# Score products of a two-layer backbone: two batches of small matmuls a head in place of four, three adaLN steps behind each

## The chip, the cores and the metric

The kernel runs on one core of a Trainium2 chip. The metric is the device time of one execution in microseconds (us), the median of several runs. The engines are named as the profile names them: PE is TensorE's matmul, PEld its weight load, DVE is VectorE, ACT is ScalarE, POOL is GpSimd, SP is SyncE, which issues the weight DMAs.

## The reference

A latent stream of 512 tokens and a context of 256 tokens go through two layers of width 1024. Each layer normalises, applies an adaLN modulation (shift, scale, gate from a conditioning vector), runs a mixer that is 2048 wide, and adds the gated result. Layer 0 is a bidirectional HGRN2 recurrence with 16 heads of 128 channels, layer 1 a bidirectional RG-LRU. The change touches layer 0 alone:

```python
q, v, zf, zb, g = jnp.split(hh @ w_in, 5, axis=-1)
f = lb + (1.0 - lb) * jax.nn.sigmoid(z)          # forget gate, one per direction; key = 1 - f
scores = jnp.einsum('bhtk,bhsk,bhtsk->bhts', qc, kc, decay)
o = einsum('bhts,bhsv->bhtv', scores, vc) + einsum('bhtk,bhkv->bhtv', qc * exp(b), S)
S = exp(b_last) * S + einsum('bhsk,bhsv->bhkv', kc * exp(b_last - b), vc)
shift, scale, gate = jnp.split(silu(c) @ ada_w[i] + ada_b[i], 3, axis=-1)
```

## The kernel before

All 768 tokens are kept with channels on the partitions, in 6 chunks of 128. The big projections are done in fp32 split into a high and a low part, three matmuls per product (lines 311 to 313; line 381 for v). A weight tile of 512 KB arrives by DMA in one of three `raw` buffers, ACT rounds it to `hi` (line 129), and DVE takes the rest as `lo` (line 130).

Inside a head the decayed scores of a chunk come from a tree of 7 levels (`NLEV`). At level l the blocks of B = 2^l tokens are paired, and the matmuls of `products` multiply the keys of one block with the queries of its neighbour, decayed up to their border. `KK` holds the keys and `QQ` the queries of both directions, and behind each level DVE multiplies both in place by decay products `T` (lines 502 and 509). `kt` is a gathered copy of KK on ACT (line 416). An odd level also gathers the queries, into `qt` (lines 416, 490, 491), and an even one reads QQ in place. Levels 0 to 5 take 24 matmuls of 128x32 each, level 6 takes 12 of 128x64. They use a part of PE's columns each (`tile_position`), while every other matmul of the head uses the whole array. `dg`, also 24 small matmuls, is the diagonal.

The four batches of a head are dg with level 0, levels 1 and 2, levels 3 and 4, levels 5 and 6. Each product has its own PSUM bank out of a pool of four (`aps`), from which the tiles `ada`, `adat`, `kT`, `U`, `o` and `pm` also come. `scores` moves products away: DVE's copy_predicated into D for levels 0 to 4 (line 468), ACT copies into `A` for levels 5 and 6 (line 473, 4 and 2 of them), and four copies from D into A (line 477).

`interleave` runs head h together with a filler, mostly the input projections (`in_0` to `in_3`) of head h+1. In odd heads the filler also has the v projection for two heads, in even heads from 2 on the output projection `o`. `prep` gathers level 0's `kt_0` of the next head ahead of that head, and makes its kd and QQ.

`ada_block` is the side work. One block has four steps of 4 matmuls (line 230), each on a 512 KB weight tile of its own; with the fourth ACT copies the bank to `blk` (line 236), then PE transposes it (`adat`, line 240) and DVE adds. The side work has two blocks in heads 0 and 1 and six in heads 9 to 14. Behind each of the four batches stands `next(side)`, one step; what is left of a block runs at the head's end.

The order on each engine is set by a scheduler that works on the recorded program: within each engine, instructions run in the order that it leaves, and a waiting one holds up those behind it. Names in the rows: `lv_5` is level 5's bank, `kT` the transposed keys, `hi`, `lo` and `raw` weights, `sg` a sigmoid, `h_hi` and `h_lo` the normalised input.

Of the kernel before, what the change touches and what calls it, by code (L numbers as in the profile page):

```python
# [9 lines left out]
AF = mybir.ActivationFunctionType  # L10
# [3 lines left out]
P = 128  # L14
# [7 lines left out]
NC = NT // P  # L22
# [22 lines left out]
def view(t, off, dims):  # L45
    a = t[:]
    if isinstance(a, Nothing):
        return a
    return bass.AP(tensor=a.tensor, offset=a.offset + off, ap=[a.ap[0]] + [list(d) for d in dims])
# [119 lines left out]
def build(tc, ins, out, plan):  # L169
    nc = tc.nc  # L170
    PE, V, A = nc.tensor, nc.vector, nc.scalar
# [7 lines left out]
    def dtile(name):  # L179
        return dps.tile([P, 512], F32, name=name, tag="d")  # L180

    def atile(name):
        return aps.tile([P, 512], F32, name=name, tag="a")
# [135 lines left out]
    l0 = ExitStack()  # L319
    p0 = lambda name, bufs=1: l0.enter_context(tc.tile_pool(name=name, bufs=bufs))  # L320
    qp, kdp, tp, ap_, sp, rp = p0("qp"), p0("kdp"), p0("tp"), p0("ap"), p0("sp"), p0("rp")
    qqp, kkp, gsp, ktp, qtp = p0("qqp", 2), p0("kkp", 2), p0("gsp", 2), p0("ktp", 3), p0("qtp", 2)
    vp, tmp = p0("vp", 3), p0("tmp", 4)
    halves = (slice(0, HN), slice(HN, NT))
    st = [{} for _ in range(NH)]
# [4 lines left out]
    def tmpt(name):  # L330
        return tmp.tile([P, HN], F32, name=name, tag="tmp")
# [81 lines left out]
    def gather(KK, kt, B):  # L413

        n = NT // (2 * B)
        A.activation(view(kt, 0, [[2 * B, n], [B, 2], [1, B]]), view(KK, 0, [[2 * B, n], [NT + B, 2], [1, B]]), AF.Copy)  # L416
# [12 lines left out]
    def hgrn(h, side):  # L429

        s = st[h]
        KK, QQ, kt = s["KK"], s["QQ"], s["kt"]
        At = ap_.tile([P, NC, P], F32, name=f"A{h}", tag="A")
        D = tmpt(f"D{h}").rearrange("p (c t) -> p c t", t=64)[:, :, :32]

        dg = atile(f"dg{h}")
        for c in range(NC):
            for g in range(4):  # L440
                t = slice(P * c + 32 * g, P * c + 32 * g + 32)
                PE.matmul(dg[32 * g:32 * g + 32, 32 * c:32 * c + 32], lhsT=s["kd"][:, t], rhs=s["q"][:, t],
                          start=c == 0, stop=c == NC - 1, skip_group_check=True, tile_position=(0, 32 * g))

        def products(l, kt, qt):
            B = 1 << l
            ps = atile(f"lv{h}_{l}")
            w = 64 if B == 64 else 32
            for c in range(NC):
                for g in range(P // w):  # L450
                    o = P * c + w * g
                    if qt is not None:
                        rhs = qt[:, o:o + w]
                    elif B < 32:
                        rhs = view(QQ, o, [[2 * B, 16 // B], [NT + B, 2], [1, B]])
                    elif g % 2 == 0:
                        rhs = QQ[:, 1, o + w:o + 2 * w]
                    else:
                        rhs = QQ[:, 0, o - w:o]
                    PE.matmul(ps[w * g:w * g + w, w * c:w * c + w], lhsT=kt[:, o:o + w], rhs=rhs, start=c == 0,  # L460
                              stop=c == NC - 1, skip_group_check=True, tile_position=(0, w * g))
            return ps

        def scores(l, ps):
            w = 64 if l == 6 else 32
            psv = ps[:, :w * NC].rearrange("p (c t) -> p c t", c=NC)
            if l < 5:
                V.copy_predicated(D, masks[:, l][:, None, :].to_broadcast([P, NC, 32]), psv)
            else:
                for g in range(P // w):  # L470
                    q = slice(w * g, w * g + w)
                    k = slice(w * (g ^ 1), w * (g ^ 1) + w)
                    A.activation(At[q, :, k], psv[q], AF.Copy)
            if l == 4:
                for g in range(4):
                    q = slice(32 * g, 32 * g + 32)
                    A.activation(At[q, :, q], D[q], AF.Copy)

        T = s["T0"]
        waiting = None  # L480
        for l in range(NLEV):
            B = 1 << l
            n = NT // (2 * B)
            m = NT // B
            first = l % 2 == 1
            if first:
                qt = qtp.tile([P, NT], F32, name=f"qt{h}_{l}", tag="qt")
                if B == 32:

                    A.activation(view(qt, 0, [[2 * B, n], [1, B]]), view(QQ, NT + B, [[2 * B, n], [1, B]]), AF.Copy)  # L490
                    A.activation(view(qt, B, [[2 * B, n], [1, B]]), view(QQ, 0, [[2 * B, n], [1, B]]), AF.Copy)  # L491
                else:
                    gather(QQ, qt, B)
                waiting = (l, kt, qt)
            else:
                pss = [(waiting[0], products(*waiting))] if waiting else []
                pss.append((l, products(l, kt, None)))
                next(side, None)
                if l == 0:
                    A.activation(D, dg[:, :32 * NC].rearrange("p (c t) -> p c t", c=NC), AF.Copy)  # L500
            kv = view(KK, 0, [[2 * B, n], [NT + B, 2], [1, B]])
            V.tensor_tensor(kv, kv, view(T, 1, [[2, n], [m - 1, 2], [0, B]]), ALU.mult)  # L502
            if l < NLEV - 1:
                kt = ktp.tile([P, NT], F32, name=f"kt{h}_{l + 1}", tag="kt")
                gather(KK, kt, 2 * B)
            T2 = tp.tile([P, 2, n], F32, name=f"T{l + 1}_{h}", tag=f"T{l + 1}")
            V.tensor_tensor(T2, view(T, 0, [[m, 2], [2, n]]), view(T, 1, [[m, 2], [2, n]]), ALU.mult)
            qv = view(QQ, 0, [[2 * B, n], [NT + B, 2], [1, B]])
            V.tensor_tensor(qv, qv, view(T, m + 1, [[2, n], [-m - 1, 2], [0, B]]), ALU.mult)  # L509
            if not first:  # L510
                for x in pss:
                    scores(*x)
            T = T2
            yield 4.0 - 0.3 * l + (1.5 if l == 0 else 0)

        for dr, cs in ((0, (0, 1, 2)), (1, (0, 1)), (0, (3, 4)), (1, (3, 4, 5))):
            ps = atile(f"kT{h}_{dr}_{cs[0]}")
            for i, c in enumerate(cs):
                PE.matmul(ps[:, P * i:P * i + P], lhsT=KK[:, dr, P * c:P * c + P], rhs=ident, is_transpose=True,
                          start=i == 0, stop=i == len(cs) - 1, skip_group_check=True)  # L520
# [7 lines left out]
        for part in ((0, 3), (3, 5)):  # L528
            for dr in range(2):
                ps = atile(f"U{h}_{dr}_{part[0]}")  # L530
                for i in range(part[0], part[1]):
                    c = chain[dr][i]
                    PE.matmul(ps[:, P * (i - part[0]):P * (i - part[0]) + P], lhsT=KK[:, dr, P * c:P * c + P],  # L533
                              rhs=Vt[:, c], start=i == part[0], stop=i == part[1] - 1, skip_group_check=True)
                for i in range(part[0], part[1]):
# [3 lines left out]
                    else:  # L539
                        c = chain[dr][i]  # L540
# [9 lines left out]
        parts = halves if h < NH - 1 else segs  # L550
        pos, sqs = [], []
        for half, c_ in enumerate(parts):
            ps = atile(f"o{h}_{half}")
            cs = range(c_.start // P, c_.stop // P)
            pos.append(ps[:, :P * len(cs)])
            for i, c in enumerate(cs):
                t = slice(P * c, P * c + P)
# [6 lines left out]
                for j, (a, b) in enumerate(ops):  # L564
                    PE.matmul(po, lhsT=a, rhs=b, start=i == 0 and j == 0, stop=c == cs[-1] and j == len(ops) - 1,  # L565
                              skip_group_check=True)
# [17 lines left out]
        for half, c in enumerate(parts):  # L584
            g = s["gs"][:, c]
# [52 lines left out]
    wi, first = {}, {}  # L638
# [52 lines left out]
    def chain_(gens):  # L691
        for g in gens:
            yield from g
# [13 lines left out]
    def extra(h):  # L707
        if h in (1, 2):
            return [ada_block(0, 3 + h)]
        return [ada_block(1, h - 10)] if h >= 10 else []  # L710

    for h in range(NH):
        if h == 0:
            fill, total = [v_item(0), in_item(0, 3), head_in(1)], 54700.0
        elif h < NH - 1:
            fill, total = [head_in(h + 1)], 45300.0 if h < NH - 2 else 23500.0
        else:
            fill, total = [in_item(h, 3), out_item((h - 3, h - 2, h - 1))], 31400.0
        side = chain_(extra(h + 1) if h < NH - 1 else [])
        interleave(hgrn(h, side), HW, chain_(fill), total)  # L720
        run_all(side)
# [13 lines left out]
    first = [[(w, dtile(f"rc{e}")[:, :CTX]) for e, w in enumerate(wx)]]  # L735
# [172 lines left out]
    s = rt[j]  # L908
# [7 lines left out]
    pss = []  # L916
    for d in range(DK):
        ps = (dtile if d < 4 else atile)(f"ro{j}_{d}")
# [14 lines left out]
    for i in range(2):  # L933
        c = slice(H * i, H * i + H)
        cx = slice(CTX + H * i, CTX + H * i + H)
        for d in range(DK):
            ps = pss[d][:, c] if d < 5 else (dtile if i else atile)(f"ro{j}_{d}_{i}")[:, :H]
# [6 lines left out]
    for i, rs in enumerate(rsf):  # L944
        c = slice(H * i, H * i + H)
        cx = slice(CTX + H * i, CTX + H * i + H)
        for k in range(DK):
            o = fin[i][k // 4][:, k % 4]
# [81 lines left out]
```

## Time and profile before

| | |
|---|---|
| runs | 1584.18, 1584.83, 1586.97 us; median 1584.83 |
| profiled execution | 1585.53 us, span 1583.7 us, granted clock 0.986 of full speed on average |
| PE busy | 1530.8 us, 97% of the span |
| PEld, DVE, ACT, POOL busy | 90%, 76%, 57%, 1% |
| chain of work that ended last | PE 87%, DVE 8%, ACT 2% |

The span runs from the first to the last instruction. The profiled execution took 0.70 us more than the median and 1.8 us more than its own span. Heads 2 to 14 last about 63 us each: head 9's dg begins at 651.85 us and head 10's at 717.70.

### The profile page before, as it was taken

To read this page: it belongs to the slowest core of one execution; us is meant where nothing else is said; L and a number is where in the kernel's file an instruction comes from. 1 tells how busy PE (TensorE), PEld (TensorE's weight loads), DVE (VectorE), ACT (ScalarE), POOL (GpSimd) and SP (SyncE) were. 2 spreads that over 40 slices of the span, in tenths; PEclk is the share of its full clock that TensorE was granted. 3 is DMA by queue.
4 is the path that set the end of the run, shared out by engine and by line. 5 is a ranking of instruction groups with operands and counts; after the bars stand their busy time and mean duration, and the time that the engine had idled before them with its cause. 6 is when DMAs were issued, how large, how long until landed. Compare 5 with 4: busy or idle time off the path is not lost.

```text
span 1583.7 us, 34061 instructions
## 1 busy us (share of the span) xinstructions
PE 1530.8 (97%) x14740; PEld 1429.7 (90%) x14740; DVE 1208.6 (76%) x1867; ACT 903.9 (57%) x1423; POOL 11.8 (1%) x16
## 2 busy tenths in 40 slices
PE   5999999999999999999999999998999999999995
PEld 3899999999999999999999999987888888888884
DVE  4767678768867878767866876787668797797898
ACT  4554554555544554554445555654578577667874
POOL 0000000000000000000000000001000000000001
PEclk9999999999999999999999999998999999999997
DMA  8231211111211211223222131201222212221211
GB/s 317 91 121 54 95 55 41 55 54 30 80 41 42 68 45 51 81 69 103 70 92 73 54 120 56 94 15 54 66 68 67 89 59 67 94 78 59 76 54 53
DMA packets 33861, 116.80 MB, mean 74 GB/s; under 512 B 3632, under 2 KB 6064, under 8 KB 33712
## 3 DMA queue, kind: packets, MB, share of 16 engines
q1 hardware_dynamic: 32192, 113.26, 22.5%
q8 instruction: 116, 1.90, 0.5%
q10 hardware_dynamic: 1520, 1.37, 0.3%
q14 instruction: 33, 0.27, 0.1%
HBM read 112.52 MB, written 2.10 MB: 72 GB/s over the span
## 4 chain that ended last, share of the span: by engine, by line
PE 87%; DVE 8%; ACT 2%; issue 1%; POOL 0%; DMA 0%; POOLq 0%; DVEq 0%; ACTq 0%
PE in L311 12%; PE in L312 11%; PE in L313 11%; PE v L381 9%; PE lv L460 4%; PE o L565 4%; PE r L313 3%; PE r L311 3%; PE r L312 3%; PE o L311 3%; PE o L312 3%; PE o L313 3%; PE U L533 2%; PE gt L311 2%; PE gt L312 2%; PE gt L313 2%
## 5 line engine op out<-in xcount | busy, mean ns | idle before, releaser
L311 PE MATMUL in<-h_hi,hi 128*128 128x384 f32 x1024 | 350.4, 343 | 3.4 <-ACT h_hi L304 2.8
L312 PE MATMUL in<-h_lo,hi 128*128 128x384 f32 x1024 | 345.8, 338 | 0.3 <-DVE h_lo L305 0.3
L313 PE MATMUL in<-h_hi,lo 128*128 128x384 f32 x1024 | 344.6, 337 | 0.0
L130 DVE TENSOR_TENSOR lo<-raw,hi 128x1024 fp32r<-128x1024 f32 x160 | 195.8, 1225 | 85.9 <-ACT hi L129 85.6
L129 ACT ACTIVATE hi<-raw 128x1024 fp32r<-128x1024 f32 x160 | 168.1, 1057 | 110.5 <-PE in L312 49.3
L311 PEld LDWEIGHTS in<-h_hi,hi 128*128 128x128 f32 x1024 | 192.9, 189 | 16.8 <-issue 9.9
L312 PEld LDWEIGHTS in<-h_lo,hi 128*128 128x128 f32 x1024 | 193.1, 189 | 2.8 <-issue 1.6
L313 PEld LDWEIGHTS in<-h_hi,lo 128*128 128x128 f32 x1024 | 192.6, 188 | 0.8 <-issue 0.4
L509 DVE TENSOR_TENSOR QQ<-QQ,T 128x768 f32<-128x768 f32 x112 | 117.7, 1051 | 20.7 <-ACT qt L491 20.5
L313 PE MATMUL r<-h_hi,lo 128*128 128x512 f32 (+1 forms) x344 | 123.8, 360 | 3.8 <-DVE lo L130 3.8
L416 ACT ACTIVATE kt<-KK 128x768 f32<-128x768 f32 x112 | 102.5, 915 | 40.8 <-DVE KK L502 33.1
L502 DVE TENSOR_TENSOR KK<-KK,T 128x768 f32<-128x768 f32 x112 | 117.3, 1047 | 9.7 <-ACT kt L416 8.2
L312 PE MATMUL r<-h_lo,hi 128*128 128x512 f32 (+1 forms) x344 | 123.1, 358 | 0.0
L311 PE MATMUL r<-h_hi,hi 128*128 128x512 f32 (+1 forms) x344 | 123.0, 358 | 0.0
L337 ACT ACTIVATE sg<-in 128x384 f32<-128x384 f32 x128 | 61.5, 482 | 100.7 <-PE in L313 100.5
L381 PE MATMUL v<-hi,h_hi 128*128 128x256 f32 x384 | 111.3, 290 | 0.0
L381 PE MATMUL v<-hi,h_lo 128*128 128x256 f32 x384 | 107.4, 280 | 0.0
L381 PE MATMUL v<-lo,h_hi 128*128 128x256 f32 x384 | 107.3, 279 | 0.0
L588 DVE RECIPROCAL sq<-sq 128x384 f32<-128x384 f32 x30 | 76.3, 2546 | 21.1 <-ACT sq L582 20.9
L405 DVE SCALAR_TENSOR_TENSOR x<-o,ada,x 128x256 f32<-128x256 f32 (+1 forms) x184 | 82.1, 486 | 11.3 <-PE o L313 10.8
L311 PE MATMUL o<-rhi,hi 128*128 128x384 f32 (+2 forms) x240 | 85.3, 357 | 1.8 <-DVE lo L130 1.2
L311 PE MATMUL gt<-xh,hi 128*128 128x384 f32 x256 | 85.6, 337 | 0.8 <-ACT xh L790 0.4
(207 smaller groups left out, 3280.1 us busy)
## 6 DMA issues: line engine op xcount, KB each, us to landing
raw<-in_hgw_dram SPq DMA_DIRECT2D x64, 512.0 KB, 3.6
raw<-in_ada_dram SPq DMA_DIRECT2D x48, 512.0 KB, 3.8
raw<-in_rgi_dram SPq DMA_DIRECT2D x32, 512.0 KB, 3.9
raw<-in_hgv_dram SPq DMA_DIRECT2D x16, 512.0 KB, 3.5
raw<-in_hgo_dram SPq DMA_DIRECT2D x16, 512.0 KB, 3.6
raw<-in_rgg_dram SPq DMA_DIRECT2D x16, 512.0 KB, 3.6
raw<-in_rgo_dram SPq DMA_DIRECT2D x16, 512.0 KB, 3.9
x<-in_x_dram SPq DMA_DIRECT2D x8, 384.0 KB, 5.9
```

What stands on the lines that cost most here:

```text
L129: self.nc.scalar.activation(hi, r, AF.Copy)
L130: self.nc.vector.tensor_tensor(lo, r, hi.bitcast(F32), ALU.subtract)
L311: PE.matmul(ps, lhsT=wh, rhs=xh, start=first and i == 0, stop=False, skip_group_check=skip)
L312: PE.matmul(ps, lhsT=wh, rhs=xl, start=False, stop=False, skip_group_check=skip)
L313: PE.matmul(ps, lhsT=wl, rhs=xh, start=False, stop=last and i == n - 1, skip_group_check=skip)
L381: PE.matmul(ps, lhsT=xh[:, kk, t], rhs=w[:, k], start=part == 0 and k == 0 and i == 0 and c % 2 == 0, stop=part == 1 and k == 3 and i == 2 ...
L405: V.scalar_tensor_tensor(xs, ps[:, a - c.start:b - c.start], gate[:, d, 1 - j:2 - j], xs, ALU.mult, ALU.add)
L416: A.activation(view(kt, 0, [[2 * B, n], [B, 2], [1, B]]), view(KK, 0, [[2 * B, n], [NT + B, 2], [1, B]]), AF.Copy)
L460: PE.matmul(ps[w * g:w * g + w, w * c:w * c + w], lhsT=kt[:, o:o + w], rhs=rhs, start=c == 0, stop=c == NC - 1, skip_group_check=True, til ...
L502: V.tensor_tensor(kv, kv, view(T, 1, [[2, n], [m - 1, 2], [0, B]]), ALU.mult)
L509: V.tensor_tensor(qv, qv, view(T, m + 1, [[2, n], [-m - 1, 2], [0, B]]), ALU.mult)
L588: V.reciprocal(rs, rs)
```

## The change

The products of a head now come in two batches. The first is the diagonal with levels 0, 1 and 2, in two PSUM banks; the second is levels 3 to 6, in three banks: levels 3 and 4 share one, level 5 and level 6 have one each. Levels 0, 1, 3, 4 and 5 gather their queries into a `qt`; levels 2 and 6, the last of each batch, read QQ. So there are two more gathers a head on ACT. The buffers of `kt` go from 3 to 5, those of `qt` from 2 to 3. Behind each batch stand up to three steps of the side work. The scores of a batch are moved away behind the level on which it ended. Line numbers behind line 440 move by up to 10: line 460 becomes 459, 468 becomes 467, 473 becomes 472.

```diff
-    qqp, kkp, gsp, ktp, qtp = p0("qqp", 2), p0("kkp", 2), p0("gsp", 2), p0("ktp", 3), p0("qtp", 2)
+    qqp, kkp, gsp, ktp, qtp = p0("qqp", 2), p0("kkp", 2), p0("gsp", 2), p0("ktp", 5), p0("qtp", 3)
...
-        def products(l, kt, qt):
+        def products(l, kt, qt, ps, first):
...
-            first = l % 2 == 1
-            if first:
+            if l not in (2, 6):
                 qt = qtp.tile([P, NT], F32, name=f"qt{h}_{l}", tag="qt")
...
-                waiting = (l, kt, qt)
+                waiting.append((l, kt, qt))
+                pss = []
             else:
-                pss = [(waiting[0], products(*waiting))] if waiting else []
-                pss.append((l, products(l, kt, None)))
-                next(side, None)
-                if l == 0:
-                    A.activation(D, dg[:, :32 * NC].rearrange("p (c t) -> p c t", c=NC), AF.Copy)
+                banks = [atile(f"lv{h}_{l}_{i}") for i in range(2 if l == 2 else 3)]
+                parts = [b[:, n_ * i:n_ * i + n_] for b in banks for i in range(2)]
+                if l == 2:
+                    diagonal(parts[0])
+                    parts = parts[1:]
+                else:
+                    parts[3] = banks[2][:, :2 * n_]
+                pss = []
+                for i, x in enumerate(waiting + [(l, kt, None)]):
+                    products(*x, parts[i], i == (1 if l == 2 else 0) or x[0] in (5, 6))
+                    pss.append((x[0], parts[i]))
+                if l == 2:
+                    A.activation(D, banks[0][:, :n_].rearrange("p (c t) -> p c t", c=NC), AF.Copy)
+                for _ in range(3):
+                    next(side, None)
+                waiting = []
...
-            if not first:
-                for x in pss:
-                    scores(*x)
+            for x in pss:
+                scores(*x)
```

The scheduler's order moves with it. The program has 82 stretches of small matmuls on PE before and 64 after; 13 in each lie in the start, ahead of the heads. Three places follow, each from before and then from the change.

On PE, head 9 from the fourth ada step on, before (`adat` is the transpose of its block, `dg` the next head's diagonal):

```order
L460 MATMUL lv_6_8142<-QQ_7315,kt_6_8086 64x64 x12
L230 MATMUL ada_0_7722<-raw_8031,sc 32x256 x4
L381 MATMUL v_0_8100<-hi_8033,h_hi 128x256
...
L313 MATMUL in_3_1_8445<-h_hi,lo_8283 128x384
L240 MATMUL adat_0_8473<-cst,blk_0_8165 128x2 x4
L442 MATMUL dg_8483<-q_7747,kd_8092 32x32 x24
L460 MATMUL lv_0_8508<-QQ_8091,kt_0_8093 32x32 x24
L230 MATMUL ada_1_8533<-raw_8280,sc 32x256 x4
```

and with the change (`lv_6_0` to `lv_6_2` are the second batch's banks; 8 v matmuls stand between the ada step and `adat`, and the repeated ones are left out here):

```order
L459 MATMUL lv_6_1_8073<-qt_5_8037,kt_5_8003 32x32 x24
L459 MATMUL lv_6_2_8074<-QQ_7269,kt_6_8041 64x64 x12
L230 MATMUL ada_0_7896<-raw_7965,sc 32x256 x4
L381 MATMUL v_0_8055<-hi_7967,h_hi 128x256
...
L381 MATMUL v_0_8055<-lo_7968,h_hi 128x256
L240 MATMUL adat_0_8171<-cst,blk_0_8169 128x2 x4
L381 MATMUL v_0_8055<-hi_7967,h_lo 128x256
```

The transpose moved from the end of the head, some 200 rows behind the fourth step, to the ninth row behind it.

On ACT, the same place before (`kt_0` is the next head's first gather, `blk` the copy that `adat` reads):

```order
L337 ACTIVATE sg_2_1_8078<-in_2_1_8053 128x384
L473 ACTIVATE A_7670<-lv_5_8117 32x6x32 x4
L416 ACTIVATE kt_0_8093<-KK_7815 128x768
L236 ACTIVATE blk_0_8165<-ada_0_7722 128x512
L473 ACTIVATE A_7670<-lv_6_8142 64x6x64 x2
```

and with the change:

```order
L337 ACTIVATE sg_2_1_8033<-in_2_1_8008 128x384
L416 ACTIVATE kt_0_8048<-KK_7767 128x768
L472 ACTIVATE A_7683<-lv_6_1_8073 32x6x32 x4
L236 ACTIVATE blk_0_8169<-ada_0_7896 128x512
L472 ACTIVATE A_7683<-lv_6_2_8074 64x6x64 x2
```

`kt_0` and the four level-5 copies changed places; `blk` stands behind both, as before.

On ACT, head 9 between the two batches before (`hi` rounds a weight that PE waits for):

```order
L337 ACTIVATE sg_1_0_7841<-in_1_0_7816 128x384
L416 ACTIVATE kt_4_7945<-KK_7055 128x768
L416 ACTIVATE qt_3_7942<-QQ_7315 128x768
L416 ACTIVATE kt_5_8042<-KK_7055 128x768
L129 ACTIVATE hi_8157<-raw_8103 128x1024
L337 ACTIVATE sg_1_1_7938<-in_1_1_7913 128x384
L337 ACTIVATE sg_2_0_7977<-in_2_0_7952 128x384
```

and with the change (`hi_7911` is the weight of the projection `in_2`, `hi_7967` that of v):

```order
L507 ACTIVATE D_7684<-lv_2_0_7797 128x6x32
L416 ACTIVATE kt_5_8003<-KK_7013 128x768
L416 ACTIVATE kt_6_8041<-KK_7013 128x768
L416 ACTIVATE qt_3_7957<-QQ_7269 128x768
L416 ACTIVATE qt_4_8000<-QQ_7269 128x768
L129 ACTIVATE hi_7911<-raw_7903 128x1024
L129 ACTIVATE hi_7967<-raw_7909 128x1024
L337 ACTIVATE sg_1_1_7953<-in_1_1_7928 128x384
```

Both weights stand behind the gathers of levels 3 and 4. On SP, the weight of `in_2` stands behind the block's first three ada tiles in the list of DMAs, which fill the three raw buffers.

On ACT, the end of head 2 before (no side work here):

```order
L129 ACTIVATE hi_2731<-raw_2723 128x1024
L337 ACTIVATE sg_2_1_2703<-in_2_1_2678 128x384
L473 ACTIVATE A_2318<-lv_5_2752 32x6x32 x2
L416 ACTIVATE kt_0_2718<-KK_2456 128x768
L473 ACTIVATE A_2318<-lv_5_2752 32x6x32 x2
L473 ACTIVATE A_2318<-lv_6_2777 64x6x64 x2
L521 ACTIVATE KK_1649<-kT_0_0_2817 128x384
L521 ACTIVATE KK_1649<-kT_1_0_2822 128x256
```

and with the change:

```order
L129 ACTIVATE hi_2679<-raw_2671 128x1024
L337 ACTIVATE sg_2_1_2651<-in_2_1_2626 128x384
L416 ACTIVATE kt_0_2666<-KK_2408 128x768
L416 ACTIVATE qt_0_3080<-QQ_2664 128x768
L472 ACTIVATE A_2320<-lv_6_1_2701 32x6x32 x4
L472 ACTIVATE A_2320<-lv_6_2_2702 64x6x64 x2
L530 ACTIVATE KK_1593<-kT_0_0_2820 128x384
```

A second gather of the next head, `qt_0`, stands ahead of the copies that free the second batch's banks. On PE the third tile of `kT` takes the bank of `lv_6_2`.

## Rows read from the trace of the kernel before

**Rows 1.** The page: busy time by engine (share, instructions); the chain by engine.

```profile
PE 1530.8 (97%) x14740; PEld 1429.7 (90%) x14740; DVE 1208.6 (76%) x1867; ACT 903.9 (57%) x1423; POOL 11.8 (1%) x16
...
PE 87%; DVE 8%; ACT 2%; issue 1%; POOL 0%; DMA 0%; POOLq 0%; DVEq 0%; ACTq 0%
```

**Rows 2.** Stretch: length, busy PE, PEld, DVE, ACT, POOL, granted clock, DMA share, GB/s.

```profile
210.00:1031.00 821.00, 820.98 (x9723) 796.80 (x9722) 626.51 (x1011) 428.48 (x729) 0.00 (x0) 1.00 0.21 66
1031.00:1064.00 33.00, 29.92 (x512) 26.95 (x512) 29.22 (x56) 17.64 (x33) 0.00 (x0) 1.00 0.06 18
1091.00:1093.00 2.00, 0.56 (x3) 0.12 (x1) 1.90 (x3) 1.64 (x3) 1.92 (x2) 1.00 0.00 0
1093.00:1104.00 11.00, 9.73 (x46) 9.64 (x47) 7.99 (x16) 4.26 (x9) 0.36 (x1) 0.53 0.13 48
```

**Rows 3.** Waits in head 15, 1030 to 1064 us: total, times, longest.

```profile
PE lv L460 <- ACT qt L416: 2.5, 2, 1.6
```

**Rows 4.** Timeline of PE, head 9: start, duration, around levels 1 and 2.

```profile
665.01 0.34 PE L311 MATMUL in<-h_hi,hi 128*128 128x384 f32 x1
...
665.88 0.34 PE L313 MATMUL in<-h_hi,lo 128*128 128x384 f32 x1
666.15 0.63 PE L460 MATMUL lv<-qt,kt 128*32 128x32 f32 x48
...
667.61 0.44 PE L311 MATMUL in<-h_hi,hi 128*128 128x384 f32 x1
667.89 0.34 PE L312 MATMUL in<-h_lo,hi 128*128 128x384 f32 x1
```

**Rows 5.** Timeline of DVE, head 9, behind the same batch.

```profile
666.84 0.48 DVE L344 TENSOR_SCALAR T<-sg,lbt 128x384 f32<-128x384 f32 x1 [1.71 <-ACT sg L337]
667.23 0.37 DVE L468 COPY_PREDICATED D<-masks,lv 128x192 f32<-128x192 uint8 x1
667.50 0.35 DVE L345 TENSOR_SCALAR KK<-T 128x384 f32<-128x384 f32 x1
...
668.90 0.95 DVE L502 TENSOR_TENSOR KK<-KK,T 128x768 f32<-128x768 f32 x1
669.77 0.95 DVE L509 TENSOR_TENSOR QQ<-QQ,T 128x768 f32<-128x768 f32 x1
```

**Rows 6.** Timeline of ACT, head 9, the same stretch.

```profile
668.75 0.85 ACT L416 ACTIVATE qt<-QQ 128x768 f32<-128x768 f32 x1 [1.09 <-DVE QQ L509]
...
671.98 1.06 ACT L129 ACTIVATE hi<-raw 128x1024 fp32r<-128x1024 f32 x1 [1.19 <-DMA raw<-in_hgv_dram]
```

**Rows 7.** Timeline of PE, head 9, levels 5 and 6 with the fourth ada step.

```profile
684.79 0.64 PE L230 MATMUL ada<-raw,sc 128*32 128x256 f32 x8
685.36 0.39 PE L381 MATMUL v<-hi,h_hi 128*128 128x256 f32 x1
685.59 0.28 PE L381 MATMUL v<-lo,h_hi 128*128 128x256 f32 x1
685.71 0.28 PE L381 MATMUL v<-hi,h_lo 128*128 128x256 f32 x1
```

**Rows 8.** Timeline of ACT, head 9, the same stretch.

```profile
684.05 1.32 ACT L473 ACTIVATE A<-lv 32x192 f32<-32x192 f32 x4 [0.70 <-PE lv L460]
685.40 1.22 ACT L416 ACTIVATE kt<-KK 128x768 f32<-128x768 f32 x1
686.64 0.60 ACT L236 ACTIVATE blk<-ada 128x512 f32<-128x512 f32 x1
```

**Rows 9.** Timeline of DVE, head 9, the same stretch.

```profile
684.66 0.36 DVE L345 TENSOR_SCALAR KK<-T 128x384 f32<-128x384 f32 x1
```

**Rows 10.** Timeline of PE, head 2: the transposed keys.

```profile
244.86 1.25 PE L519 MATMUL kT<-cst,KK 128*128 128x128 f32 x10
```

**Rows 11.** Timeline of ACT, head 2, ahead of them.

```profile
243.82 1.67 ACT L473 ACTIVATE A<-lv 32x192 f32<-32x192 f32 x4
```

**Rows 12.** Timeline of DVE, head 2, the same stretch.

```profile
242.11 0.35 DVE L345 TENSOR_SCALAR KK<-T 128x384 f32<-128x384 f32 x1
```

More of the change, by code (lines that the diff above doesn't have):

```diff
@@ L434, in hgrn, with diagonal @@
         D = tmpt(f"D{h}").rearrange("p (c t) -> p c t", t=64)[:, :, :32]
[L438 to L443, printed above, removed]
-        def products(l, kt, qt):
+        def diagonal(ps):
+            for c in range(NC):
+                for g in range(4):
+                    t = slice(P * c + 32 * g, P * c + 32 * g + 32)
+                    PE.matmul(ps[32 * g:32 * g + 32, 32 * c:32 * c + 32], lhsT=s["kd"][:, t], rhs=s["q"][:, t],
+                              start=c == 0, stop=c == NC - 1, skip_group_check=True, tile_position=(0, 32 * g))
+        def products(l, kt, qt, ps, first):
             B = 1 << l
-            ps = atile(f"lv{h}_{l}")
             w = 64 if B == 64 else 32
@@ L459, in products @@
                         rhs = QQ[:, 0, o - w:o]
-                    PE.matmul(ps[w * g:w * g + w, w * c:w * c + w], lhsT=kt[:, o:o + w], rhs=rhs, start=c == 0,
-                              stop=c == NC - 1, skip_group_check=True, tile_position=(0, w * g))
-            return ps
+                    PE.matmul(ps[w * g:w * g + w, w * c:w * c + w], lhsT=kt[:, o:o + w], rhs=rhs,
+                              start=first and c == 0, stop=c == NC - 1, skip_group_check=True,
+                              tile_position=(0, w * g))
         def scores(l, ps):
             w = 64 if l == 6 else 32
-            psv = ps[:, :w * NC].rearrange("p (c t) -> p c t", c=NC)
+            psv = ps.rearrange("p (c t) -> p c t", c=NC)
             if l < 5:
@@ L479, in hgrn @@
         T = s["T0"]
-        waiting = None
+        waiting, n_ = [], 32 * NC
         for l in range(NLEV):
```

## The prediction

> **What bounds the kernel now.** I read the page first. PE is busy for 97% of the span and makes up 87% of the chain of waits [rows 1]; no other engine comes near. Then the busy time by stretch: from 210 to 1031 us, heads 2 to 14, PE works 820.98 of 821 us at the full granted clock, while ACT works 428.48 us, about half [rows 2]. So PE has no wait there to lose. What the change can win in these heads is PE work alone, and every new wait of PE is added in full. Only at the end of layer 0 does PE wait for scores: head 15 has no filler, and two of its products wait 2.5 us together for a query gather [rows 3]. Then I read the timeline around a batch on PE, and last the order of the instructions, because each engine runs in it and one late instruction holds up all behind it.
>
> **A. Fewer batches.** A change between full-array and small matmuls costs time. In head 9 the last full matmul before levels 1 and 2 starts at 665.88, the batch .27 later instead of .174, the spacing of full matmuls (five from 665.01 to 665.88), so .10 is lost going in. The first full matmul behind starts at 667.61, the second .28 later: .11 lost coming out [rows 4]. Between lie 96 small records and one ada step. An ada step takes .57 to the next full matmul where it stands behind levels 5 and 6 [rows 7], so the 96 records took 667.61 - .57 - 666.15 = .89, 9.3 ns each. Of that .57 I put .44 on the eight records and .12 on emptying the array, which no row separates. A change and its return is then .21 to .33 us; I take .33, the end that holds the emptying as well. The order has 64 batches where there were 82, so the gain is 18 x .33 = 5.9 us (3.8 at the lower price). It isn't two in each head, because the scheduler cuts level 3's products in pieces in the adaLN heads. The number of products and ada steps is the same. The two added gathers a head are on ACT, which has room on average; where they are late they appear in C and D. In head 15 there are nine batches for eight, but the first starts from an earlier gather; I take nothing, between a loss of 1 us and a gain of 1.5, the longest wait there now being 1.6 [rows 3].
>
> **B. The weight behind the gathers.** In the heads with side work, ACT now has qt_3 and qt_4 ahead of the weight of in_2. Take head 9 and let the first batch begin where levels 1 and 2 did, at 666.15. On PE it lasts .33 + 192 x 9.3 ns + three ada steps of .44 = 3.4; 24 full matmuls of .174 follow, and PE wants the weight at 666.15 + 7.6 = 673.75. DVE begins as before at 666.84 with L344 (.39 to the next), does two products into q (estimated at .5 each from L344's own .48), L345 and a copy (.27 each), a KK and a QQ multiplication (.87 each by their spacing) [rows 5]: 670.5. Then qt_3 on ACT takes .85 [rows 6], to 671.35, while DVE does two copies and a KK, to 671.9. The next QQ multiplication takes .95, to 672.85, qt_4 .85, and the rounding of the weight 1.06 [rows 6]: 674.75. PE waits 1.0 by this sum; I take .9, since the waits overlap the drain. By the same working: three heads (9, 11, 13) x .9, two (10, 12) x 1.2, because `o` lies differently there, head 14 1.0, head 1 .45, head 0 .65. That makes 7.2 us. The bounds are 0, if DVE reaches the QQ multiplication 1 us sooner, and 12, if the weight of v, rounded next in another 1.06, is waited for as well. The DMA of in_2's weight can start only when the first ada matmuls have freed a buffer; I count on its landing before qt_4 ends.
>
> **C. The transpose of an adaLN block.** Before, `adat` stood 200 rows behind the fourth step. Now nine rows. In head 9 the fourth step started at 684.79 [rows 7]; the batch has 70 records more (half of level 3, all of level 4), .65, so it starts at 685.44. The next full matmul starts .57 later, the one after that .23 later, then .117 each [rows 7]: eight of them end at 687.06, and PE wants the transpose. `blk` isn't there. On ACT kt_0, four level-5 copies and then `blk` stand in a row. kt_0 needs L345, which ran at 684.66 [rows 9], and now has a copy_predicated of .27 [rows 5] between L344 and itself: 684.93 + .35 = 685.3. Then 1.22 for kt_0, 1.32 for the copies, .60 for `blk` [rows 8]: 688.45. PE stops for 1.4 us, with its own in-order queue behind it: v, kT, U and the next head's input. Heads 9, 11, 13: 4.2. In heads 10 and 12 six matmuls of .174 stand between, not eight, but a shorter tail on ACT: 1.15 each. Head 1 has both level-6 copies ahead of `blk` as well, 2.2; head 0 has no kt_0 ahead, .5; head 14 has neither, 0. Together 9.2 us. The bounds are 0 and 13, the latter if the copies start only when the whole batch is done.
>
> **D. The banks for kT.** The even heads 2, 4, 6, 8 have no side work, but qt_0 now stands behind kt_0 on ACT ahead of all copies of the second batch. In head 2, kt_0 can start when L345 is done, 242.46 [rows 12], and takes 1.22; qt_0, with the same short runs, another 1.22; the four level-5 copies 1.32 [rows 8]; the two of level 6 about 1.0 (what is left of 1.67 [rows 11] after half of 1.32): 247.25. PE began kT at 244.86 [rows 10]; with 96 more records in the batch ahead, .9, that is 245.75. Five of the ten transposes later, half of 1.25 less .1 of overlap, it wants the third bank: 246.3. It is free at 247.35 with the hand-over, so PE waits 1.1 us, 4.4 in four heads. Lower bound 0 (copies first), upper 1.5 each, if all of qt_0 and a late L345 count. The odd heads 3, 5, 7 have the longer v filler there and .3 to .5 us to spare by the same sum.
>
> The Trainium skill, in "TensorEngine Tiling (Array Packing)", section Performance Considerations, speaks against the change: tiling speeds up TensorE but not the evacuation of PSUM, so the "PSUM copy may become bottleneck". The trace of before doesn't show it, PE being busy without a gap [rows 2]; by that rule the odd heads would pay D's price as well, 3 x 1.1 us more.
>
> **The sum.** -5.9 + 7.2 + 9.2 + 4.4 = +14.9 on the profiled execution's 1585.53, 1600.4. That execution took .7 more than the median of the runs, so I predict 1599.7 us, 0.9% slower. What is late next, where a wait goes: B's wait shifts PE and not ACT, which makes C's wait no shorter, since kt_0 hangs on PE's own in_2_1.
>
> **Rivals.**
> *The covers hold.* ACT is half idle [rows 2]; if it does kt_0 and the copies some 1.4 us earlier than I count, because the semaphores let it start on the first piece of a product, and DVE reaches QQ early, all waits vanish and A alone is left: 1584.83 - 5.9 = 1578.9. It decides at one place: whether kt_0 in head 9 starts before 684. Against it: kt_0 started at 685.40 before, and its input is DVE's, which the change moves later.
> *Only the transpose waits.* B and D are covered (the rounding of a weight starts only .9 too late, D is 1.1): -5.9 + 9.2 gives 1588.1. For it: B and D rest on chains of six to ten instructions, C on four.
> *The waits are half.* Each of B, C and D at half: -5.9 + 10.4 = +4.5, 1589.3; at a quarter, -.7, no change.
> *All banks bind.* The odd heads pay as well: 1603.
> *The clock falls.* Behind PE's idle 1.4 us from 1091 to 1093, the granted clock was .53 for 11 us, the 1.2 GHz level for most of it; in head 15, with single waits up to 1.6 [rows 3], it stayed at 1.00 [rows 2]. Head 1's 2.2 us lies above both. One such fall costs about 11 x .47 = 5 us: 1605; in each of the five middle heads as well, far more.
>
> **How the numbers follow.** The forecast, three kinds of wait in about these sizes, .50 (its own range 1594 to 1605). All banks bind .07, the clock falls .07. Only the transpose, or all at half, .14. A quarter, within .2% (3.2 us, what a measurement of this kernel can tell from none), .09. The covers hold, .13. Slower by over .2%: .50 + .07 + .07 + .13 = .77 (.01 of the halves falls under the limit); same .10; faster .13. The range from 1582 to 1606 leaves out most of the covers and the clock's far end, about .2, and spans A's and the waits' bounds as far as these chances go.
>
> **What would show it.** The profile after should have some 14 us of PE idle between 210 and 1031 us where there was none, most before `adat` with `blk` (ACT L236) as its releaser, at 1.4 us in heads 9, 11 and 13; about 1 us before in_2 or v in heads 9 to 13, released by `hi`; and about 1 us within kT in heads 2, 4, 6, 8, released by the level-6 copies. PE's busy time should fall little. I am wrong if PE shows no idle time there, if `adat` doesn't wait, or if the granted clock in heads 1 to 13 is below 1.00. The batch of levels 3 to 6 should be .9 us longer than that of levels 5 and 6 was.

## The result

The changed kernel takes 1621.51 us (median of 6 runs, 1616.93 to 1628.68) where the kernel before takes 1585.36 (6 runs, 1584.18 to 1586.97): a ratio of 1.023, 95% interval 1.0214 to 1.0246. The prediction was 1599.7 us, in a range from 1582 to 1606. It had the right side and the wrong size: 36 us slower, not 15. The profiled execution took 1620.35 us, its span 1618.6.

The page after, against [rows 1]: busy time by engine, DMA queues (packets, MB, share), the chain by engine.

```profile
PE 1535.0 (95%) x14740; PEld 1435.0 (89%) x14740; DVE 1205.1 (74%) x1867; ACT 926.6 (57%) x1455; POOL 11.8 (1%) x16
...
q8 instruction: 116, 1.90, 0.5%
...
PE 79%; DVE 12%; ACT 6%; issue 2%; DMA 1%; POOL 0%; POOLq 0%; ACTq 0%; DVEq 0%
```

PE runs the same 14740 matmuls as before, but its share of the chain fell from 87% to 79%. The waits of PE from 200 to 1060 us, up to the end of head 14, where there were none before [rows 2] (who waited for what: us in total, times, longest):

```profile
PE lv L459 <- issue: 10.1, 5, 2.8
PE adat L240 <- ACT blk L236: 5.7, 5, 1.2
PE in L311 <- ACT hi L129: 4.9, 5, 1.1
PE kT L528 <- ACT A L472: 1.7, 3, 0.6
PE v L381 <- ACT hi L129: 1.3, 1, 1.3
```

The first line is the one that nobody had on the list. Its releaser is "issue": no semaphore that the profile shows held PE up. The others are C, B and D of the prediction; together they make 13.6 us, where it had announced some 14. Against [rows 2], the same stretch, two short ones behind a wait, and one head without any:

```profile
210.00:1031.00 821.00, 797.34 (x9444) 776.22 (x9443) 603.89 (x976) 427.20 (x724) 0.00 (x0) 0.99 0.20 63
490.00:492.00 2.00, 2.00 (x8) 2.00 (x7) 2.00 (x4) 0.85 (x1) 0.00 (x0) 0.53 0.04 8
708.00:710.00 2.00, 2.00 (x13) 2.00 (x13) 1.83 (x5) 1.98 (x4) 0.00 (x0) 0.64 0.17 68
555.00:617.00 62.00, 62.00 (x762) 61.65 (x762) 44.14 (x66) 35.22 (x61) 0.00 (x0) 1.00 0.17 52
```

Between 210 and 1031 us PE is idle for 24 us, against 0.02 before, and the granted clock is 0.99. From 490 to 492 it is .53, the 1.2 GHz level for most of the stretch, right behind a stop of 2.11 us inside a batch; from 708 on it is .64, behind a wait for the transpose. The trace has four such falls in the heads, each of 3.4 us at half of full speed, so I put 1.7 us on each, an estimate. A granted clock below 1.00 there was one of the prediction's signs of being wrong. Head 7, at 555 to 617, has no wait at all.

**What the batch shows.** PE's timeline in head 5, first batch (start, duration, idle before; a record is one matmul instruction, and its weight load is another):

```profile
418.46 0.60 PE L442 MATMUL lv<-q,kd 128*32 128x32 f32 x46
...
418.91 1.00 PE L459 MATMUL lv<-qt,kt 128*32 128x32 f32 x92
...
419.76 0.54 PE L459 MATMUL lv<-QQ,kt 128*32 128x32 f32 x38
423.07 0.27 PE L459 MATMUL lv<-QQ,kt 128*32 128x32 f32 x8 [2.77 <-issue]
```

The batch starts, 184 records run at 9 ns each, and then, in the midst of level 2, PE stands still for 2.77 us. The next eight records are of the same level, from the same tiles, into the same bank. Six such stops lie in the heads (one in head 0, two each in heads 5 and 6, one in head 9), 12.0 us in all. I counted PE's instructions in the trace (weight loads, matmuls, semaphore instructions): ahead of the one that comes after the stop stand 1217, 8897, 9409, 10433, 10945 and 14785. Each is 193 + a multiple of 256; why the rest is 193 and not 0 isn't shown. The queue `q8 instruction` moves 1.90 MB in 116 packets, 16 KB each, and 29,650 instructions on PE in 116 packets are about 256 in one. So PE's instructions come in blocks of 256, and PE stops at a block's border. The packets' own times show what it waits for. From just before the stop of head 5 until its end a single DMA packet moved, one of that queue (packets, MB, share, 420.10 to 423.07 us):

```profile
q8 instruction: 1, 0.02, 3.0%
```

It took from 420.13 to 421.54 us, and PE went on at 423.07. The other five stops end 1.3 to 1.6 us behind the end of such a packet too, as do all 48 stops in the traces of the changed kernel and of runs 1 to 6 (1.2 to 1.6). The six stops end 3.5 to 4.3 us after PE was about 48 instructions ahead of the border before; at all other borders the two moments lie 3.4 us or more apart by themselves, and there is no stop. In the kernel before they lie 7.3 us or more apart everywhere. In full-array work 256 instructions last 22 us. In a batch they are 128 records, 1.2 us. A batch of at most 104 records, as before, can't hold two borders; one of 192 can, and whether it does depends on where the border falls. The Trainium skill, in "Runtime: NRT & Kernel Launch", section "Instruction fetch mechanics", says that instructions come in blocks of 16 KiB with 256 in each, as here, and that the cost of crossing a border is mostly hidden. In the changed kernel's batches it isn't: the measured stops, 1.6 to 2.8 us, decide.

**The predicted waits** are there too. Head 9, the transpose on PE, then ACT and DVE, against [rows 7 to 9]:

```profile
704.12 0.64 PE L230 MATMUL ada<-raw,sc 128*32 128x256 f32 x8
...
705.62 0.28 PE L381 MATMUL v<-lo,h_hi 128*128 128x256 f32 x1
707.08 1.05 PE L240 MATMUL adat<-cst,blk 128*128 128x2 f32 x8 [1.18 <-ACT blk L236]
```

```profile
703.99 1.21 ACT L416 ACTIVATE kt<-KK 128x768 f32<-128x768 f32 x1 [1.84 <-DVE KK L345]
705.10 1.31 ACT L472 ACTIVATE A<-lv 32x192 f32<-32x192 f32 x4
706.43 0.60 ACT L236 ACTIVATE blk<-ada 128x512 f32<-128x512 f32 x1
```

```profile
703.34 0.37 DVE L467 COPY_PREDICATED D<-masks,lv 128x192 f32<-128x192 uint8 x1
703.60 0.35 DVE L345 TENSOR_SCALAR KK<-T 128x384 f32<-128x384 f32 x1
```

PE is through with its eight v matmuls at 705.9 and stands for 1.18 us, because kt_0, the copies and `blk` follow each other on ACT, and kt_0 waits for L345, which the copy_predicated at 703.34 has pushed back. The weight in head 10, on PE and on ACT:

```profile
761.17 0.44 PE L311 MATMUL in<-h_hi,hi 128*128 128x384 f32 x1 [0.94 <-ACT hi L129]
```

```profile
759.33 0.85 ACT L416 ACTIVATE qt<-QQ 128x768 f32<-128x768 f32 x1 [1.42 <-DVE QQ L519]
760.08 1.99 ACT L129 ACTIVATE hi<-raw 128x1024 fp32r<-128x1024 f32 x2
```

The rounding starts the moment that the second qt gather ends. And kT in head 2, against [rows 10, 11]:

```profile
251.02 0.82 PE L528 MATMUL kT<-cst,KK 128*128 128x128 f32 x5
252.41 0.77 PE L528 MATMUL kT<-cst,KK 128*128 128x128 f32 x5 [0.57 <-ACT A L472]
```

```profile
247.83 1.20 ACT L416 ACTIVATE kt<-KK 128x768 f32<-128x768 f32 x1 [1.97 <-DVE KK L345]
248.94 1.20 ACT L416 ACTIVATE qt<-QQ 128x768 f32<-128x768 f32 x1
250.04 2.32 ACT L472 ACTIVATE A<-lv 32x192 f32<-32x192 f32 x6
```

kt_0, qt_0 and six copies run without a gap from 247.83 to 252.36; the third tile waits for the last of them.

### The profile page after: what moved, and what is told of

Its sections match the earlier page's. It is cut to its first block, busy times and chain, and to the rows that moved or that the text cites. A ratio compares the mean times of both kernels' runs of the same rounds, so it can differ in the third digit from the quotient of the medians.

```text
span 1618.6 us, 33986 instructions
## 1 busy us (share of the span) xinstructions
PE 1535.0 (95%) x14740; PEld 1435.0 (89%) x14740; DVE 1205.1 (74%) x1867; ACT 926.6 (57%) x1455; POOL 11.8 (1%) x16
## 4 chain that ended last, share of the span: by engine, by line
PE 79%; DVE 12%; ACT 6%; issue 2%; DMA 1%; POOL 0%; POOLq 0%; ACTq 0%; DVEq 0%
PE in L311 10%; PE in L312 10%; PE in L313 10%; PE v L381 8%; PE o L574 4%; PE r L313 3%; PE r L311 3%; PE r L312 3%; PE o L311 3%; PE o L312 2%; PE o L313 2%; DVE lo L130 2%; PE lv L459 2%; PE U L542 2%; PE gt L311 2%
```

## The experiments

Theory F says that PE runs out of instructions where two borders of blocks of 256 fall into one batch or close behind it. A row of small matmuls is 4 instructions (two records, each with its weight load), a full-array row of the projections 2, a tiny matmul of the start 4, so the order of a program alone gives the place of every border; the numbers in the expectations come from that and from 3.7 us.

**1. Move the borders.** 36 tiny matmuls more in the start; a few rows of the start changed places with it, the order in the heads stayed.

```diff
-        for m in range(4):
+        for m in ([0] * 36 if l == 0 and b == 0 else []) + [0, 1, 2, 3]:
             PE.matmul(pt[:, 2 * m:2 * m + 2], lhsT=blk[:, P * m:P * m + P], rhs=sel,
```

> The changed kernel with 36 more tiny matmuls (144 PE instructions) in the start, ahead of the heads; nothing else differs, the order of all other instructions is kept. Theory F (instruction fetch): in the changed kernel PE stopped six times inside a batch, each time at an instruction whose number on PE leaves the same rest when divided by 256. PE's instructions come in blocks of 256 and a block is there some 3.7 us after it was asked for, about 48 instructions ahead of a block's border; a batch of small matmuls uses 256 instructions in 1.2 us, so two borders in one batch stop it for up to 2.4 us. Moved by 144 instructions, the borders give 17 stops worth about 31 us (12 us before), none left in heads 5 and 6, and new ones in heads 1, 3, 4, 7, 8 and 10 to 14; time 1638 to 1652 us. Rival G (the stop belongs to the head, by a buffer or semaphore that the profile does not show): the same six stops in heads 0, 5, 6 and 9, 12 us, time 1617 to 1628 us.

Measured: 1656.76 us (ratio to before 1.0442, 1.0421 to 1.0463). Waits of PE over all heads, of those with no releaser:

```profile
PE lv L459 <- issue: 24.9, 14, 2.6
...
PE o L313 <- issue: 1.1, 1, 1.1
PE ada L230 <- issue: 1.1, 1, 1.1
...
PE in L313 <- issue: 0.4, 1, 0.4
```

17 stops, 27.5 us, for the 17 and 31 expected, each ahead of an instruction with the rest 193 again. Heads 5 and 6 have none; head 3, quiet before, has two. The first of them, as it stands on PE:

```profile
309.02 0.56 PE L459 MATMUL lv<-QQ,kt 128*32 128x32 f32 x41
312.18 0.26 PE L459 MATMUL lv<-QQ,kt 128*32 128x32 f32 x5 [2.59 <-issue]
```

G is out: the same program with the same gathers, banks and side work stops elsewhere. The time is 5 us above the range. Of its distance to the changed kernel 15.5 us are stops, and the trace has eight falls of the clock in the heads for four. But the added matmuls cost time themselves, which the expectation left out. In the start the transpose's row is now

```profile
24.86 15.88 PE L240 MATMUL adat<-cst,blk 128*128 128x2 f32 x80 [0.72 <-ACT blk L236]
```

where the changed kernel has 8 records in 1.05 us; the granted clock is .50 from 26.4 to 50.2 us, and head 0's first U matmul starts at 132.94 us for 120.22. (U, behind the transposed keys of a head, is what the head adds to the state S.)

**2. The transpose back at the head's end.**

```diff
-                for _ in range(3):
+                for _ in range(3 if l == 2 else 1):
                     next(side, None)
```

> The changed kernel with one step of side work behind the second batch in place of three, so that the transpose of an adaLN block runs at the head's end, as before the change. Theory: the eight waits of 0.5 to 1.8 us before the transpose (8.0 us) go, and so do two of the four falls of the clock, those behind such a wait (3.5 us); the six fetch stops, the waits for weights (7.1 us) stay: 1608 to 1613 us. Rival: the transpose only shows a wait that the kT, U and S work behind it would have had anyway; then PE waits for kT or U in heads 9 to 13 and the time falls by less than 3 us, to 1618 or more.

Measured: 1610.36 us (1.0152, 1.0137 to 1.0167), 11 us less. The waits for the transpose (seven, not eight) are gone and little took their place; the longest of PE's waits over the heads:

```profile
PE lv L459 <- issue: 10.7, 6, 2.2
PE in L311 <- ACT hi L129: 5.1, 6, 1.1
```

No fall of the clock is left in its heads, where the changed kernel had four. Two of those four stood behind stops, and the stops are still there, so not all of the 11 us is the transpose's.

**3. Two steps of side work behind each batch.**

```diff
-                for _ in range(3):
+                for _ in range(2):
                     next(side, None)
```

> The changed kernel with two steps of side work behind each batch in place of three, the transpose at the head's end. The weight of in_2 then has a raw buffer before the first batch, and its rounding stands ahead of the gathers of levels 3 and 4 on ACT. Theory: the waits for the transpose (8.0 us), the waits for weights (7.1 us), and the clock's falls behind the transpose (3.5 us) go, and the scheduler no longer cuts level 3 in pieces (52 batches for 64, 12 x 0.33 = 4 us); the fetch stops stay at 12 to 13 us. Time about 1599 us (1594 to 1604). Rival: the weights are late whatever the side work does, because ACT has two gathers more a head; then in waits for hi as before, and the time is 1606 or more.

Measured: 1603.12 us (1.0115, 1.0098 to 1.0132). No wait for `hi` is left, so B was the raw buffers and the order that follows from them, not the number of gathers. What remains is mostly stops and banks:

```profile
PE lv L459 <- issue: 12.4, 6, 3.5
PE kT L528 <- ACT A L472: 2.3, 4, 0.6
PE o L312 <- issue: 1.9, 1, 1.9
```

So of the 36 us some 18 went with the side work. The stops stay. By the order and 3.7 us, an estimate that no run tested, no shift of the borders would remove them: two batches a head leave stops of 7 us or more wherever the borders fall.

**4. Three shorter batches.** Batches of 96, 144 and 120 records; the table says which level ends a batch and how many steps stand behind.

```diff
-            if l not in (2, 6):
+            if l not in ENDS:                      # (0, 3, 6)
...
-                for _ in range(3):
+                for _ in range(STEPS[l]):          # {0: 1, 3: 2, 6: 1}
                     next(side, None)
```

> Three batches a head: the diagonal with level 0; levels 1 to 3; levels 4 to 6, with one, two and one steps of side work behind them and the transpose at the head's end. No batch is longer than 144 products' records plus two steps, so that two block borders fall into one only rarely: by theory F one or two stops, 1.5 us in all. 67 batches for the 82 before the change: -15 x 0.33 = -5 us. If no other wait appears: 1580 to 1584 us, faster than before the change (1585) by 0.1 to 0.3%. Rival G2: the waits came from batches fewer than four and from gathers, not from their length; then this kernel too has stops inside batches, some 6 us of them, and waits for banks: 1590 us or more.

Measured: 1600.64 us (1.0091, 1.0075 to 1.0106); the expected gain wasn't there. There is one stop, 1.2 us, as expected, so G2's stops didn't come; its waits for banks did, as waits of kT:

```profile
PE kT L529 <- ACT A L472: 12.6, 11, 1.4
PE in L311 <- issue: 1.2, 1, 1.2
```

ACT at the end of head 3 shows them: kt_0, the level-6 copies, D's four, and only then the level-5 copies that free the bank.

```profile
306.73 1.22 ACT L416 ACTIVATE kt<-KK 128x768 f32<-128x768 f32 x1 [1.71 <-DVE KK L345]
307.86 0.97 ACT L472 ACTIVATE A<-lv 64x384 f32<-64x384 f32 x2
309.63 1.49 ACT L476 ACTIVATE A<-D 32x192 f32<-32x192 f32 x4 [0.80 <-DVE D L467]
311.12 1.32 ACT L472 ACTIVATE A<-lv 32x192 f32<-32x192 f32 x4
```

**5. A bank for each of levels 4 to 6, D's copies later.** The edit against run 4; of the table's line only the last entry is shown.

```diff
-  6: ({4: (0, 0), 5: (0, 1), 6: (1, 0)}, 2)
+  6: ({4: (0, 0), 5: (1, 0), 6: (2, 0)}, 3)
...
-            if l == 4:
-                for g in range(4):
-                    q = slice(32 * g, 32 * g + 32)
-                    A.activation(At[q, :, q], D[q], AF.Copy)
```

(the four copies then stand behind the transposed keys)

> The three batches of the last experiment, with levels 4, 5 and 6 in a PSUM bank each (level 4 shared one with level 5) and the four copies from D into A written behind the transposed keys, so that the banks which kT takes come free earlier. Theory: of the run's 15.5 us of new PE idle in heads 0 to 14, 14.3 were kT and U behind ACT's copies of level 5, held up by kt_0, the level-6 copies and D's copies; by the order on ACT the copies now end before PE wants the bank, these waits go, and two stops inside batches (1.9 us) stay: 1581 to 1586 us, from 0.3% faster than before the change to the same. Rival: three batches leave ACT too much to do at a head's end whatever the banks, and kT or U still wait 6 us or more: 1591 us or more.

Measured: 1586.61 us (1.0007, 0.9997 to 1.0017): 14 us less than run 4, level with the kernel before and .6 us above the range. PE's waits up to head 14, all of them:

```profile
PE U L542 <- ACT KK L527: 1.5, 1, 1.5
PE ada L230 <- issue: 1.1, 1, 1.1
```

The rival is out; which of the two edits freed the banks isn't separated. By head 13 the kernel was 3.0 us ahead of the one before; it lost 2.3 of them in heads 14 and 15, which have little filler.

**6. The batch's length alone.** The kernel before, with its four batches, its gathers and its banks.

```diff
-        for c in range(NC):
+        for c in [0] * 12 + list(range(NC)):
             for g in range(4):
```

> The kernel before the change with 48 of the diagonal's first small matmuls repeated in each head, so that the first batch of its four is as long (192 records) as the first of the changed kernel; nothing else is changed, gathers, banks and side work are as before. The added work alone is 48 x 18.6 ns x 16 heads = 14.3 us. Theory F (instruction blocks of 256): ten stops, worth 20 us, in heads 2 to 5, 7 and 10 to 14, all of them 1 to 2.3 us, and some falls of the clock behind them at 1.7 us each: 1618 to 1632 us. Rival (a stop needs two batches a head, the added gathers or shared banks): no stop inside a batch, 1598 to 1602 us.

Measured: 1630.98 us (1.0285, 1.027 to 1.0301). Ten stops, 24.7 us in all, in heads 3 to 6, 8 and 11 to 15 (the expectation's head numbers are each one too low), each ahead of an instruction with the rest 193. Four are longer than expected, 2.7 to 3.5 us: there the packet of instructions began 2.0 to 2.8 us after PE was 48 instructions ahead of the border before, in the changed kernel's six stops 1.0 to 1.5 us. Why it began late isn't settled. PE's waits up to head 14, and head 6:

```profile
PE lv L460 <- issue: 20.9, 8, 3.5
PE in L312 <- issue: 1.8, 1, 1.8
```

```profile
476.90 1.40 PE L442 MATMUL dg<-q,kd 128*32 128x32 f32 x142
...
478.15 0.61 PE L460 MATMUL lv<-QQ,kt 128*32 128x32 f32 x38
482.29 0.33 PE L460 MATMUL lv<-QQ,kt 128*32 128x32 f32 x8 [3.53 <-issue]
```

A batch of 192 records stops PE in a kernel that has nothing else of the change. The added work shows by itself in the heads without a stop, as .8 us a head, 13 in all. The stops, and six falls of the clock behind them up to head 14, one twice as long as the others, make up the rest of the 46 us; head 15 hid most of its own stop behind a wait that it had anyway.

**7 and 8. Four batches in heads 14 and 15, and the borders moved.** Run 5 with four batches in these two heads (that part of the edit isn't shown) and 13 tiny matmuls that move the borders by 52 instructions, in run 7 as in run 1, in run 8, shown here, at PE's beginning, where it waits for its first weights:

```diff
+        for _ in range(13 if l == 0 and b == 0 else 0):
+            PE.matmul(ps[:, 0:2], lhsT=ident, rhs=sel, start=True, stop=True, skip_group_check=True)
         for j in range(4):
             w = wget("ada", l, b, j)
```

> The last three-batch kernel with two repairs: heads 14 and 15 keep four batches, as before the change (they had lost 2.3 us there), and 13 more tiny matmuls in the start move the instruction blocks by 52, so that by theory F no border pair falls into a batch (one stop of 1.1 us before). Theory: what is left is the saving of fewer batches, 3.0 us by head 13 in that run plus the 1.1 of the stop; the start costs 0 to 1 us for the added matmuls: 1580.5 to 1583 us where the kernel before has 1585.5, faster by 0.15 to 0.3%. Rival: the stops are only partly a matter of where the borders fall, and one or two come back elsewhere: 1584 to 1587 us.

> As the last run, but the 13 added matmuls stand at PE's very beginning, where it waits some 14 us for its first weights anyway, and no longer ahead of the first projection. Theory: the last run gained 4.1 us from head 0 to head 15 and lost 2.7 us ahead of head 0 by the added matmuls; with that loss gone and no stop inside a batch: 1580 to 1582.5 us, faster than the kernel before by 0.2 to 0.35%. Rival: the 2.7 us came from another order in the start and not from the matmuls themselves, or the gain of fewer batches is eaten up behind head 15: 1584 us or more.

Run 7: 1584.66 us (0.9995, 0.9985 to 1.0004), above the range: there is no stop in any batch, but of the 4.1 us that the heads gained 2.7 were lost ahead of head 0, whose U came that much later. Run 8: 1581.75 us (0.9972, 0.9961 to 0.9983), faster than the kernel before by 0.28%, in its heads PE without a gap again, as in [rows 2]:

```profile
210.00:1031.00 821.00, 820.19 (x9755) 798.11 (x9742) 626.30 (x1010) 431.47 (x742) 0.00 (x0) 1.00 0.21 66
```

## Why the prediction was wrong

What fails is a step in A and B: "the 96 records took 667.61 - .57 - 666.15 = .89, 9.3 ns each", and then, for the longer batch, ".33 + 192 x 9.3 ns". The price of a record was read from batches of at most 96 and carried to 192. In the longer ones PE runs out of instructions, six times, 12.0 us, and twice the clock fell behind such a stop, by estimate 3.4 us more. No term and no rival had these stops.

Point by point, in the profiled execution (span +34.8 us):

| term | predicted | measured |
|---|---|---|
| A, fewer batches, heads 1 to 14 | -5.9 | -3.5 |
| B, weights behind gathers | +7.2 | +7.1 in 8 waits |
| C, transpose of a block | +9.2 | +8.0 in 7 waits |
| D, banks for kT | +4.4 | +1.7 in 3 waits |
| stops inside batches | none | +12.0 in 6 |
| clock falls in the heads | a rival at .07 | +6.9 by estimate in 4, two behind a stop, two behind the transpose |
| head 0, head 15 and behind | 0 | +2.6 left over |

A is what is left of the distance from head 0's U to head 14's once waits and falls are taken out. Heads 3 and 7, without any wait, gained .8 each, .4 for each batch less; heads 10 to 13, where level 3 is cut in pieces and at most one batch is saved, lost .1 to .4, and why isn't shown. B was right to .1 us in the sum, and that is in part luck: in heads 10 and 12 PE waited .9 us for 1.2, in head 9 1.30 for .9, and there for the weight of v and not of in_2. C's working held: 1.4 forecast and 1.18 to 1.19 measured in heads 9, 11 and 13, since ACT's instructions begin before the one ahead has ended (1.11 from kt_0 to the copies for its 1.21). D was mis-sized, .57 for 1.1: two gathers and six copies one behind another took 4.5 us, not 4.8, and PE came to the third tile .8 us behind the first, not .55. In head 6 PE didn't wait at all; the stop of 1.64 us in the batch ahead had given ACT the time.

The clock's rival was right in its mechanism and wrong in its condition and its price. It set the limit above 1.6 us, from head 15, and took a fall to be 11 us long. The trace of before has a short one as well, right behind PE's waits of 1.18, .86 and .66 us at the end of layer 0, which the prediction passed over (columns as in [rows 2], the clock third from the end):

```profile
1080.00:1083.00 3.00, 3.00 (x14) 2.93 (x15) 3.00 (x7) 1.65 (x5) 1.74 (x2) 0.50 0.37 146
```

In the changed kernel falls came behind waits of 1.18, 1.64, 1.76 and 2.11 us, and none behind those of 2.77 and 1.94. The length of a wait isn't what decides. What else PE did ahead of a fall isn't settled here. The clock differs from run to run of the same program: over six executions the mean granted clock was .976 to .985 and the time 1616.93 us at .985 and 1625.04 at .976, but 1628.68 at .979, so the clock is at most a part of the changed kernel's wider spread, and no experiment isolated it. Of the 2.6 us of the last row 1.1 lie ahead of head 0's U and 1.5 behind head 14's; what they are was not traced.

The rule of the Trainium skill that the prediction weighed, "PSUM copy may become bottleneck" ("TensorEngine Tiling (Array Packing)", section Performance Considerations), came true in run 4 more than in the change. In the change the odd heads paid nothing; kT waited in heads 2, 4 and 8 alone. In run 4 kT waited 12.6 us for copies, and that was gone with a bank more and the copies from D later.

## What to carry to other kernels

Where a batch of very short matmuls grows, ask whether PE can be fed: count its instructions, put a border every 256, and look for two borders within less than some 4 us (here the stops ended 3.5 to 4.3 us after PE was 48 instructions ahead of the first). Price a batch only up to the length that a trace has shown. Work behind a batch that is read back soon, as a transpose of an evacuated bank, wants as much other work between as before, since what stands ahead of its copy on the copying engine is the real distance.

## What the hardware showed that was not expected

PE's stops at instruction numbers that leave the rest 193 by 256, 1.6 to 2.8 us in the changed kernel and up to 3.5 in run 6; so the place of a border alone moves a kernel (six stops or 17, 12.0 or 27.5 us, with 144 instructions more ahead of the heads). Falls of the granted clock to .50 for about 3.4 us, behind waits of 1.18 to 2.11 us and not behind each of them. The change to small matmuls and back cost .4 us in the quiet heads, where [rows 4] had given .21 to .33.
